# Half of the products of spectra and the filters' sums on GpSimd, the norms of some heads on ScalarE, and six more products of zeros

## The chip, the cores and the metric

The kernel runs on one core of one Trainium2 chip. The metric is the device time of one launch in microseconds, the median of 3 runs. Five engines take part: TensorE (PE for its products, PEld for its weight loads), VectorE (DVE), ScalarE (ACT), GpSimd (POOL) and SyncE (SP), which issues the loads.

## The reference

A two-layer encoder on 256 tokens of width 1024, in float32, with a memory of 256 tokens.

- Layer 0 mixes by a Hyena operator: the projected input goes through a short convolution over three neighbours, and then twice through `z = chunk * fftconv(z, filter)`. The filters come from a small network of sines over positions, and each is divided by the sum of the magnitudes of its taps. `fftconv` is a product of spectra: transform, multiply by the filter's spectrum, transform back.
- Beside it stands a cross attention of 4 heads of 128 to the memory. Queries and keys are normed head by head: each row's 128 numbers of a head are divided by the root of their mean square (`head_rms`).
- An output projection, a residual, and a SwiGLU of hidden width 2816 follow.
- Layer 1 mixes by dilated attention in three groups with the same head norms, again beside a cross attention, and ends in a mixture of 8 SwiGLU experts, of which each token takes 2.

## The kernel before

**Arithmetic.** Large products are done in three passes of a split number: each float32 operand is held as a high part (rounded by a ScalarE copy) and a low part (source minus high part, by a VectorE `tensor_tensor`, line 645, `split`). `mm3` (line 653) then does high*high, high*low and low*high. Every weight that is loaded goes through this split, in halves of 1024 columns (line 668, `weights`).

**Order of the work.** `Plan` (line 138) records every operation of the kernel. `flush` (line 588) then makes one list for nearly the whole kernel and emits it: `order` (line 397) gives each operation a due time by walking backwards through the graph, and then plays the engines forward with the durations of `cost` (line 321), taking at each engine the ready operation that is due first and for which buffers are free. So each engine's order is fixed when the kernel is built, and a changed operation or duration can change the order anywhere. Line 344 is what the planner assumes of a GpSimd `tensor_tensor`; it knows nothing of engines that hinder each other.

**The start.** `run` (line 851) sets up a tile of zeros and lets TensorE multiply it `WARM` times by itself, 128x128 in plain float32 (lines 881 to 884); these stand first on TensorE. In the trace each such product is two records. Then come the two products and the two sines of the filters' network (`taps`, line 899), which are due first on every engine, and the first dense block, the memory's keys of layer 0 (`memory`, line 1130).

**Head norms.** `heads_T` (line 748) norms the heads of a [2 x 128 tokens, 512] result that lies in PSUM, transposes them on TensorE and splits them. It is called four times: by `memory` for the keys of both layers, and by `cross` (line 802) for the queries of both. `head_norms` (line 726) does the norm: for each of two halves of the tokens one ScalarE Square over 512 columns and one VectorE reduction to 4 sums; then `rsqrt` (line 677, with a power on GpSimd over 8 columns); then for each half one VectorE product of 512 columns with the 4 factors broadcast. The dilated attention (`chunks`, line 1211) uses `head_norms` too.

**Filters and spectra.** `filters` (line 932) makes for each of the two filters the magnitudes of two tiles, adds them (line 956), and multiplies the sum by ones on TensorE to get the norm. `long_conv` (line 1043) takes the spectrum of its input and forms, for each of two halves r of the frequencies, four products of 512 columns with the filter's spectrum and from them a difference and a sum:

```python
for i, (f, g) in enumerate(((R[r], A[r]), (I[r], Dq[r]), (R[r], Dq[r]), (I[r], A[r]))):
    nc.vector.tensor_tensor(out=m[i], in0=f, in1=g, op=OP.mult)
nc.vector.tensor_tensor(out=m[0], in0=m[0], in1=m[1], op=OP.subtract)
nc.vector.tensor_tensor(out=m[2], in0=m[2], in1=m[3], op=OP.add)
```

The results are split and go back through TensorE. `long_conv` runs twice; between the two and after them stand the dense blocks of the projected input (`channels`, line 1002), whose convolution over neighbours is done by VectorE from PSUM, and whose results TensorE transposes (`channels_T`, line 1033).

Of the kernel before, what the change touches and what calls it, by code (L numbers as in the profile page):

```python
# [16 lines left out]
AF = mybir.ActivationFunctionType  # L17
OP = mybir.AluOpType
# [8 lines left out]
HD = 128  # L27
EPS = 1e-6
NB = 32
NUNIT = 33  # L30
WARM = 14


C_XQ, C_XK, C_AQ, C_AK = 0, 2, 4, 5
# [586 lines left out]
class _Kernel:  # L621
# [125 lines left out]

    def heads_T(self, ps, dst, scale=None, rms=None):

        zn = self.head_norms(ps, 0, 4, rms)  # L750
        d = dst.rearrange("p (h a t) -> p h a t", h=4, a=2)
        for a in range(2):
            p = self.bank()
            for h in range(4):
                self.tr(p[:, h * 128:(h + 1) * 128], zn[a][:, h * HD:(h + 1) * HD])
            self.split(d[:, :, a], p.rearrange("p (h t) -> p h t", h=4), scale=scale)
# [94 lines left out]
    def run(self):  # L851
# [30 lines left out]
        nc.vector.memset(idle, 0.0, kind="first")  # L882
        for _ in range(WARM):
            nc.tensor.matmul(ps[:, :128], lhsT=idle, rhs=idle, start=True, stop=True, kind="warm")
# [47 lines left out]
    def filters(self, hp, hm, w3, decay, skip, dft):  # L932

        nc = self.nc
        self.A, self.Dq, self.inv = [], [], []
        for o in range(2):
            at = slice(o * 512, (o + 1) * 512)
            P, Q, ab = [], [], []  # L940
            for t in range(2):
                pq = []
                for h, dst in ((hp, P), (hm, Q)):
                    ps = self.bank()
                    nc.tensor.matmul(ps, lhsT=h[:, t * 128:(t + 1) * 128], rhs=w3[:, at], start=True, stop=True)
                    pq.append(self.slot(512))
                    nc.vector.tensor_tensor(out=pq[-1], in0=ps, in1=decay[:, t * 512:(t + 1) * 512], op=OP.mult)
                    dst.append(pq[-1])

                mag = [self.slot(512) for j in range(2)]  # L950
                for j in range(2):
                    nc.scalar.activation(mag[j], pq[j], AF.Abs)
                ab.append(mag[0])
                nc.vector.tensor_tensor(out=ab[t], in0=mag[0], in1=mag[1], op=OP.max)
            ps, tot = self.bank(), self.slot(512)
            nc.vector.tensor_tensor(out=tot, in0=ab[0], in1=ab[1], op=OP.add)
            nc.tensor.matmul(ps, lhsT=self.ones, rhs=tot, start=True, stop=True)
            sk = self.slot(512)
            nc.vector.scalar_tensor_tensor(sk, ps, 1e-6, skip[:, at], op0=OP.add, op1=OP.mult)

            ps = self.bank()
            for j in range(4):
                nc.tensor.matmul(ps[:, j:j + 1], lhsT=tot[:, j * 128:(j + 1) * 128], rhs=self.ones[:, :1],
                                 start=True, stop=True)
            inv = self.tiny(4)
            nc.vector.tensor_scalar(inv, ps[:, :4], 1e-6, None, op0=OP.add)
            nc.vector.reciprocal(inv, inv)
            self.inv.append(inv)
            A, Dq = self.spectrum(dft, P, Q, sk)
            self.A.append(A)  # L970
            self.Dq.append(Dq)
# [71 lines left out]
    def long_conv(self, o, U, dft):  # L1043


        nc = self.nc
        R, I = self.spectrum(dft, U, U)
        A, Dq = self.A[o], self.Dq[o]
        Y = {}
        for r in (1, 0):  # L1050
            m = [self.slot(512) for i in range(4)]
            for i, (f, g) in enumerate(((R[r], A[r]), (I[r], Dq[r]), (R[r], Dq[r]), (I[r], A[r]))):
                nc.vector.tensor_tensor(out=m[i], in0=f, in1=g, op=OP.mult)
            nc.vector.tensor_tensor(out=m[0], in0=m[0], in1=m[1], op=OP.subtract)
            nc.vector.tensor_tensor(out=m[2], in0=m[2], in1=m[3], op=OP.add)
            Y[0, r], Y[1, r] = m[0], m[2]
        out = []
        for i in range(2):
            for r in range(2):
                out.append(self.pair(512))  # L1060
                self.split(out[-1], Y[i, r])
        return out
# [175 lines left out]
    def head(self, h, at, vecs, out):  # L1238

        nc = self.nc  # L1240

        bias = self.bias_of(vecs, h).rearrange("p (a s t) -> p a s t", a=2, s=4)
        q, k, v = ([at[f"{n}{g}", h] for g in range(3)] for n in "qkv")
        half = lambda p, a: p[:, a * 128:(a + 1) * 128]
        pT = self.pair(1024).rearrange("p (s a t) -> p s a t", s=4, a=2)
        for a in range(2):
            ps = self.bank()
            self.mm3(ps[:, :256], half(q[0], a), k[0], True, True)
            for g in (1, 2):
                self.mm3(ps[:, 128 + 128 * g:256 + 128 * g], half(q[g], a), half(k[g], a), True, True)  # L1250
            sc = self.slot(512)
            nc.vector.tensor_tensor(out=sc.rearrange("p (s t) -> p s t", s=4), in0=ps.rearrange("p (s t) -> p s t", s=4),
                                    in1=bias[:, a, :, ::-1], op=OP.add)
            g1 = lambda t: t.rearrange("p (z k) -> p z k", z=1)
            self.softmax_rows(g1(sc), 1, g1(sc))
            tp = self.bank()
            for s in range(4):
                self.tr(tp[:, s * 128:(s + 1) * 128], sc[:, s * 128:(s + 1) * 128])
            self.split(pT[:, :, a], tp.rearrange("p (s t) -> p s t", s=4))
        po = self.bank()  # L1260
        for s in range(2):
            self.mm3(po[:, :256], half(v[0], s), pT[:, s].rearrange("p a t -> p (a t)"), s == 0, False)
        for s in (2, 3):
            for a in range(2):
                self.mm3(po[:, a * 128:(a + 1) * 128], half(v[s - 1], a), pT[:, s, a], False, s == 3 and a == 1)
        self.split(out[:, h], po[:, :256])
# [380 lines left out]
```

## Time and profile before

| | us |
|---|---|
| median of 3 runs (lowest to highest) | 1317.12 (1317.06 to 1317.91) |
| the profiled execution, device time | 1316.6 |
| its span, first to last instruction | 1314.7 |
| PE busy | 1298.1 (99%) |
| PEld busy | 1073.8 (82%) |
| DVE busy | 1082.4 (82%) |
| ACT busy | 903.9 (69%) |
| POOL busy | 42.0 (3%), 38 instructions |

The span is 1.9 us shorter than the profiled execution's device time. The mean granted clock of TensorE over the span is 0.995 of the full one. A busy time is the time in which an engine had an instruction in work; matmuls are pipelined, and their ends are modelled, so neighbours overlap. Since all operations are emitted by one helper, nearly every row has line L301, and the operations are told apart by tile names and shapes: `b` is a PSUM bank, `s` a tile of SBUF, `tiny` a few columns of scalars, `kt` the constants, `x` the residual stream, `mhalf` the exponents of the power.

### The profile page before, as it was taken

The numbers are of one execution on the slowest core, as the hardware profiler recorded it, in microseconds if no ns is written. First come the engines' busy times: TensorE is split into PE (matmuls) and PEld (weight loads), VectorE is DVE, ScalarE is ACT, GpSimd is POOL, SyncE is SP. The second block draws the span as 40 slices with busy tenths as digits, with TensorE's granted clock in tenths as the row PEclk, the third lists the DMA queues.
The fourth block names the chain that finished last, engine by engine and source line by source line (L and its number), as shares of the span: only waits on it lengthen the run. The fifth ranks groups of instructions, "written<-read, shape, count | busy, mean of one in ns | idle before, by whom it ended". The sixth has DMA issues, their size and how long they took to land.

```text
span 1314.7 us, 16854 instructions
## 1 busy us (share of the span) xinstructions
PE 1298.1 (99%) x6236; PEld 1073.8 (82%) x6236; DVE 1082.4 (82%) x1434; ACT 903.9 (69%) x1185; POOL 42.0 (3%) x38
## 2 busy tenths in 40 slices
PE   7999999999999999999999999999999999999997
PEld 5798888888878888888888888888888888888885
DVE  7999765554578777899988999898998899989895
ACT  7455854444556565687777877777777777778884
POOL 1000000000001001000000000000000000000000
PEclk8999999999999999999999999999999999999998
DMA  9737534457434465388999998999998999999961
GB/s 364 297 129 288 225 119 140 152 186 268 166 132 173 157 212 222 115 347 330 346 411 417 336 381 323 372 421 384 359 373 308 397 380 422 336 381 370 354 264 18
DMA packets 57725, 373.82 MB, mean 284 GB/s; under 512 B 6447, under 2 KB 10627, under 8 KB 13988
## 3 DMA queue, kind: packets, MB, share of 16 engines
q1 hardware_dynamic: 56484, 368.48, 72.4%
q0 software_dynamic: 1152, 4.19, 1.8%
q8 instruction: 51, 0.84, 0.2%
q14 instruction: 38, 0.31, 0.1%
HBM read 366.86 MB, written 5.79 MB: 283 GB/s over the span
## 4 chain that ended last, share of the span: by engine, by line
PE 88%; issue 7%; DVE 3%; ACT 1%; DMA 1%; POOL 0%; POOLq 0%; ACTq 0%; DVEq 0%
PE b L301 88%; DVE s L301 3%; ACT s L301 1%; DMA out<-s,tiny 1%; DVE tiny L301 0%; POOL tiny L301 0%; POOL out L298 0%; DVE x L301 0%; POOLq L1387 0%; ACTq L301 0%; POOLq L298 0%; DVEq L301 0%
## 5 line engine op out<-in xcount | busy, mean ns | idle before, releaser
L301 PE MATMUL b<-s,s 128*128 128x512 f32 (+2 forms) x5678 | 1270.0, 382 | 6.4 <-ACT s L301 3.6
L301 PEld LDWEIGHTS b<-s,s 128*128 128x128 f32 (+1 forms) x5678 | 1009.0, 188 | 212.3 <-DVE s L301 6.7
L301 DVE TENSOR_TENSOR s<-s,s 128x1024 fp32r<-128x1024 f32 (+2 forms) x728 | 835.0, 1185 | 140.7 <-ACT s L301 137.9
L301 ACT CAST s<-s 128x1024 fp32r<-128x1024 f32 (+1 forms) x701 | 699.9, 1038 | 244.2 <-PE b L301 124.3
L301 DVE TENSOR_TENSOR s<-b,s 128x512 f32<-128x512 f32 (+5 forms) x214 | 127.6, 610 | 36.8 <-ACT s L301 32.3
L301 ACT CAST s<-b 128x512 fp32r<-128x512 f32 (+3 forms) x118 | 58.2, 502 | 55.7 <-PE b L301 53.6
L301 PE MATMUL b<-kt,s 128*128 128x128 f32 (+1 forms) x448 | 78.0, 271 | 0.4 <-ACT s L301 0.4
L301 PEld LDWEIGHTS b<-kt,s 128*128 128x128 f32 x448 | 58.6, 144 | 16.5 <-ACT s L301 1.3
L301 ACT ACTIVATE s<-b 128x512 f32<-128x512 f32 (+3 forms) x81 | 43.1, 536 | 23.7 <-PE b L301 18.6
L301 POOL TENSOR_TENSOR tiny<-tiny,mhalf 128x1 f32<-128x1 f32 (+4 forms) x23 | 28.6, 1246 | 323.3 <-DVE tiny L301 323.1
L301 ACT ACTIVATE s<-b,sm 128x256 fp32r<-128x256 f32 (+1 forms) x68 | 28.3, 484 | 13.1 <-PE b L301 12.5
L301 ACT ACTIVATE s<-b,tiny 128x256 f32<-128x256 f32 (+2 forms) x50 | 28.6, 598 | 12.3 <-PE b L301 11.7
L298 POOL DMA_INDIRECT out<-s,tiny x8 | 12.9, 1612 | 754.2 <-ACT s L301 658.5
L301 DVE SCALAR_TENSOR_TENSOR s<-b,sm,s 128x256 fp32r<-128x256 f32 (+1 forms) x72 | 31.1, 476 | 5.1 <-ACT s L301 4.9
L301 DVE TENSOR_REDUCE tiny<-s 128x4 f32<-128x512 f32 (+4 forms) x34 | 19.3, 586 | 7.7 <-ACT s L301 7.5
L301 ACT ACTIVATE s<-s,tiny 128x256 f32<-128x256 f32 (+1 forms) x32 | 18.4, 616 | 7.6 <-DVE tiny L301 7.6
L301 ACT ACTIVATE s<-x 128x512 f32<-128x512 f32 x16 | 10.1, 629 | 10.5 <-DVE x L301 9.8
L301 DVE TENSOR_TENSOR tiny<-tiny 128x1 f32<-128x1 f32 (+4 forms) x81 | 12.2, 157 | 4.5 <-POOL tiny L301 2.7
L301 PE MATMUL b<-s 128*128 128x128 f32 (+3 forms) x64 | 14.5, 349 | 1.1 <-DVE s L301 1.1
L301 ACT ACTIVATE s<-s 128x512 f32<-128x512 f32 (+2 forms) x14 | 8.2, 596 | 9.8 <-DVE s L301 9.8
L301 DVE TENSOR_TENSOR x<-b,x 128x512 f32<-128x512 f32 x12 | 8.3, 690 | 7.6 <-PE b L301 7.6
L301 DVE TENSOR_TENSOR s<-b,tiny 128x512 f32<-128x512 f32 (+3 forms) x26 | 13.7, 559 | 0.6 <-PE b L301 0.4
(67 smaller groups left out, 149.4 us busy)
## 6 DMA issues: line engine op xcount, KB each, us to landing
s<-w_moe SPq DMA_DIRECT2D x264, 1024.0 KB, 7.5
s<-w_ffn SPq DMA_DIRECT2D x33, 1024.0 KB, 4.9
s<-w_at SPq DMA_DIRECT2D x20, 1024.0 KB, 5.0
s<-w_kv SPq DMA_DIRECT2D x8, 1024.0 KB, 4.9
s<-w_hy SPq DMA_DIRECT2D x8, 1024.0 KB, 13.4
s<-w_out SPq DMA_DIRECT2D x8, 1024.0 KB, 5.3
s<-mem_t SPq DMA_DIRECT2D x4, 512.0 KB
out<-x SPq DMA_DIRECT2D x3, 512.0 KB, 2.7
```

Of the source, the lines that this page charges most:

```text
L298: self.nc.gpsimd.indirect_dma_start(out=out, out_offset=bass.IndirectOffsetOnAxis(ap=index, axis=0), in_=rows, in_offset=None, compute_op= ...
L301: getattr(getattr(self.nc, op.eng), op.fn)(*args, **kw)
```

## The change

Four edits. The number of products of zeros goes from 14 to 20. `heads_T` no longer calls `head_norms`: it squares each head by itself on ScalarE with the sum accumulated by the same instruction (8 instructions for 2), needs no VectorE reduction, and multiplies each head by its factor on ScalarE (8 instructions for VectorE's 2). The sum of the two magnitude tiles of each filter goes from VectorE to GpSimd. Of the four products of spectra the second and the fourth go to GpSimd.

```diff
-WARM = 14
+WARM = 20
     def heads_T(self, ps, dst, scale=None, rms=None):
-        zn = self.head_norms(ps, 0, 4, rms)
+        nc = self.nc
+        head = lambda t, h: t[:, h * HD:(h + 1) * HD]
+        ss = self.tiny(8)
+        for a in range(2):
+            kw = {} if rms is None else dict(scale=rms[a])
+            for h in range(4):
+                nc.scalar.activation(self.slot(HD), head(ps[a], h), AF.Square, accum_out=ss[:, 4 * a + h:4 * a + h + 1], **kw)
+        r = self.rsqrt(ss, 8, HD)
+        for a in range(2 if rms else 0):
+            nc.vector.tensor_scalar(r[:, 4 * a:4 * a + 4], r[:, 4 * a:4 * a + 4], rms[a], None, op0=OP.mult)
+        zn = [self.slot(512) for a in range(2)]
+        for a in range(2):
+            for h in range(4):
+                nc.scalar.activation(head(zn[a], h), head(ps[a], h), AF.Copy, scale=r[:, 4 * a + h:4 * a + h + 1])
         d = dst.rearrange("p (h a t) -> p h a t", h=4, a=2)
...
             ps, tot = self.bank(), self.slot(512)
-            nc.vector.tensor_tensor(out=tot, in0=ab[0], in1=ab[1], op=OP.add)
+            nc.gpsimd.tensor_tensor(out=tot, in0=ab[0], in1=ab[1], op=OP.add)
...
             for i, (f, g) in enumerate(((R[r], A[r]), (I[r], Dq[r]), (R[r], Dq[r]), (I[r], A[r]))):
-                nc.vector.tensor_tensor(out=m[i], in0=f, in1=g, op=OP.mult)
+                (nc.gpsimd if i % 2 else nc.vector).tensor_tensor(out=m[i], in0=f, in1=g, op=OP.mult)
```

## Rows read from the trace of the kernel before

**Rows 1.** Busy time by stage: us, each engine's busy time (instructions), PEclk, DMA.
```profile
24.80:33.70 8.90, 8.08 (x40) 5.23 (x39) 7.15 (x18) 8.68 (x14) 1.65 (x1) 1.00 1.02 406
33.00:130.00 97.00, 97.00 (x591) 83.26 (x590) 93.18 (x160) 51.66 (x80) 2.55 (x1) 1.00 0.61 234
62.00:84.50 22.50, 22.50 (x165) 21.36 (x163) 22.33 (x37) 10.94 (x17) 0.00 (x0) 1.00 0.14 47
```
**Rows 2.** Waits of PE from 24.9 to 1306: us, times, longest us.
```profile
PE b L301 <- DVE s L301: 1.2, 2, 0.7
PE b L301 <- ACT s L301: 0.4, 1, 0.4
```
**Rows 3.** Timeline of the start: start us, us, instruction, count [idle before].
```profile
4.78 1.17 PE L301 MATMUL b<-s 128*128 128x128 f32 x9
5.23 0.72 PE L301 MATMUL b<-s 128*128 128x128 f32 x5
6.56 0.53 DVE L301 TENSOR_SCALAR s<-b,sm 64x256 f32<-64x256 f32 x1 [2.52 <-PE b L301]
14.10 11.14 PE L301 MATMUL b<-s,s 128*128 128x512 f32 x40 [1.41 <-DVE s L301]
```
**Rows 4.** Busy time in three stretches of the start, columns as above.
```profile
6.54:9.45 2.91, 0.00 (x0) 0.00 (x0) 2.71 (x7) 1.51 (x3) 0.00 (x0) 1.00 1.04 435
11.07:17.88 6.81, 5.40 (x13) 3.72 (x13) 6.67 (x15) 6.81 (x17) 0.09 (x1) 0.50 1.01 374
17.90:24.80 6.90, 6.90 (x31) 5.69 (x31) 5.51 (x31) 4.84 (x12) 2.16 (x4) 1.00 1.02 421
```
**Rows 5.** Timeline of ACT at the first head norm.
```profile
24.88 0.69 ACT L301 ACTIVATE s<-b,tiny 128x512 f32<-128x512 f32 x1 [1.38 <-PE b L301]
...
26.99 1.15 ACT L301 ACTIVATE s<-x,tiny 128x1024 f32<-128x1024 f32 x1
```
**Rows 6.** Timeline of ACT: a Square of 128 columns; accumulating activations of 256.
```profile
503.60 0.28 ACT L301 ACTIVATE s<-b 128x128 f32<-128x128 f32 x1 [5.61 <-PE b L301]
...
130.08 0.47 ACT L301 ACTIVATE s<-b,tiny 128x256 f32<-128x256 f32 x1
...
130.53 0.47 ACT L301 ACTIVATE s<-b,tiny 128x256 f32<-128x256 f32 x1
```
**Rows 7.** Groups of DVE, 60 to 84.5: operation, shapes, count, busy us, mean ns.
```profile
L301 DVE TENSOR_TENSOR s<-s,s 128x512 f32<-128x512 f32 x12 | 7.7, 683 | 0.0
```
**Rows 8.** Groups of DVE, 24.8 to 33.8.
```profile
L301 DVE TENSOR_REDUCE tiny<-s 128x4 f32<-128x512 f32 x2 | 1.4, 686 | 2.4 <-ACT s L301 2.4
```
**Rows 9.** Timeline of the first long convolution.
```profile
67.60 3.09 DVE L301 TENSOR_TENSOR s<-s,s 128x512 f32<-128x512 f32 x5
...
81.17 3.21 DVE L301 SCALAR_TENSOR_TENSOR s<-b,tiny,s 128x255 f32<-128x255 f32 x8
...
84.50 0.63 PE L301 MATMUL b<-kt,s 128*128 128x128 f32 x4
```
**Rows 10.** Groups of POOL over the span.
```profile
L301 POOL TENSOR_TENSOR tiny<-tiny,mhalf 128x6 f32<-128x6 f32 x2 | 2.6, 1322 | 24.9 <-DVE tiny L301 24.9
...
L301 POOL TENSOR_TENSOR tiny<-tiny,mhalf 128x2 f32<-128x2 f32 x2 | 1.4, 696 | 15.9 <-DVE tiny L301 15.9
```
**Rows 11.** Timeline where POOL's power of 8 columns meets DVE.
```profile
112.39 1.22 DVE L301 TENSOR_TENSOR s<-s,s 128x1024 fp32r<-128x1024 f32 x1
112.56 2.55 POOL L301 TENSOR_TENSOR tiny<-tiny,mhalf 128x8 f32<-128x8 f32 x1 [81.81 <-DVE tiny L301]
...
406.94 1.65 POOL L301 TENSOR_TENSOR tiny<-tiny,mhalf 128x8 f32<-128x8 f32 x1 [29.44 <-DVE tiny L301]
407.10 2.35 DVE L301 TENSOR_TENSOR s<-s,s 128x1024 fp32r<-128x1024 f32 x2
```
**Rows 12.** Timeline at layer 0's cross attention: the norm's second product, first transposes.
```profile
119.36 0.68 DVE L301 TENSOR_TENSOR s<-b,tiny 128x512 f32<-128x512 f32 x1
119.47 0.60 PE L301 MATMUL b<-kt,s 128*128 128x128 f32 x4
```

## The prediction

> **What bounds the kernel now.** I read the busy times by stage first. From 33 to 130 us, the stage in which both long convolutions and both filters lie, PE is busy for all 97.00 us, and DVE for 93.18 of them; ACT has half of the stage free [rows 1]. So two engines are full side by side, and the question is which one waits for the other. The view of waits answers it: from 24.9 us to 1306 PE waits three times in all, 1.6 us together [rows 2], and the same view of 33 to 130 has no row for PE. PE is the bound, DVE runs just ahead of it. Work taken off DVE there buys nothing by itself; work added to DVE costs as soon as PE comes to wait. What an edit can still win lies in those 1.6 us and in the start, read from the timeline: DVE stands idle until the products of zeros and the first product behind them are through (6.56), and from there its queue leads to 14.10, where PE begins the first dense block after a wait of 1.41 us for DVE [rows 3]. In the start the clock also counts: PE did nothing from 6.54 to 9.45, and from 11.07 to 17.88 the granted clock was 0.50, 1.2 GHz, before it came back [rows 4].
>
> **Six more products of zeros.** Each is two records. Nine records from 4.78 and five from 5.23 end together, so four take 0.45 us, 0.112 each at full clock [rows 3]; twelve take 1.35 us. They stand first on PE, and behind them the product for the sines, DVE's sines, DVE's low parts and then the dense block at 14.10. DVE was busy for 2.71 of the 2.91 us after 6.54 [rows 4], so I find no cover: the block starts 1.35 us later. What it loses is less, since until 17.88 it ran at half the clock [rows 4]: 1.35 us of that time was worth 0.67 us of work. That holds if the clock falls as before, and I think it does: the pause of 2.9 us that stood before the fall [rows 4] is moved, not shortened. **+0.7.** Upper bound +1.35 (nothing absorbed); lower bound -1.9: the clock stays up, which gives back half of the 3.78 us from 14.10 to 17.88, and DVE fills the wait with a low part of the weights.
>
> **Head norms, four calls.** Each call takes two reductions (0.69 us) and two products (0.68) from DVE [rows 8, 12]; on a queue without pauses such an operation of 512 columns costs 0.60, five taking 3.09 with the overlap of the last [rows 9], so DVE gains 2.4 us a call. For ACT, a Square of 128 columns took 0.28 us, and accumulating activations of 256 columns with a pointer follow each other by 0.45 [rows 6]; the new Square lies between them, and I take 0.37, as 128 columns fewer than 256 save about 0.08 by the two rows. Eight make 3.0 us for 1.2 now (two of 0.60). The eight scaled copies I take at 0.33 (between the same rows), 2.6 us. So ACT gains 4.4 us of work a call, and a norm ends about 1.8 us later at its sums and 1.4 later at its copies. Of the calls, three have cover: the layer 0 queries (ACT half idle [rows 1], and the first transposes come at 119.47, in a PE queue with no wait [rows 12, 2]) and both of layer 1's, in stretches where PE waits 0.9 us in all [rows 2]. The first call has none: from 24.80 to 33.70 ACT is busy for 8.68 of 8.90 us [rows 1]. There ACT waits 1.38 us for the dense block, does the two Squares, and only then scales the second half of the rows of x (26.99) [rows 5], on which the next dense block hangs. If all eight Squares are put ahead of that, it is 1.8 us late; if it goes before them, PE's longest wait, 0.7 us, is won. With half of them ahead, 4 x 0.37 stand for 1.2: **+0.3**, bounds -0.7 and +1.8.
>
> **Sums of magnitudes and products of spectra: ten operations of 512 columns.** On DVE one takes 0.68 us [rows 7]. On GpSimd no row shows a plain one; its powers cost 0.696 us for 2 columns and 1.322 for 6 [rows 10], 0.157 a column and 0.38 fixed. Lower bound 0.68, DVE's own time for the same work; upper bound, at the power's slope, 0.38 + 512 x 0.157 = 80.8 us. A product of two tiles is nearer to DVE's row than to a power, so I take GpSimd's fixed 0.38 and, for 512 columns more, what DVE's operation of 1024 (1.22 [rows 11]) takes beyond one of 512, 0.54: 0.92 us.
>
> Does it run beside DVE? The power of 8 columns takes 1.65 us where it starts ahead of DVE's subtraction of two SBUF tiles, and 2.55 where that subtraction is already running [rows 11]: POOL waited for 0.9 us. In the other direction two such subtractions that start 0.16 us after the power take 2.35 as a pair, undisturbed [rows 11], but the power reads only 8 columns. The Trainium skill (SBUF — State Buffer, section "Who interferes with whom") says that a VectorE instruction with two SBUF inputs contends with a GpSimd instruction that reads SBUF, by a lock held for the whole instruction. The trace agrees for POOL's side; for DVE's side no row has a read long enough. By that page no product would run beside one of DVE's, by the pair at 407.10 alone all would. The skill's price (GPSIMD Engine Reference, section "Elementwise — side-by-side cycle accounting") is 1.96 times VectorE's, so an estimate of 1.34 us; the ten would then cost 13.4 us instead of 9.2.
>
> I reckon with the serial case from the rows. In the first long convolution DVE is full (22.33 of 22.50 [rows 1]), and nearly all of its work there has two SBUF inputs [rows 7, 9]. Four products leave DVE (-2.4) and block it for 4 x 0.92: +1.3 in each convolution; the two sums +0.6 together. The first norm has by then given DVE 2.4. So at 84.50, where PE's transposes follow DVE's convolution (81.17 + 3.21 = 84.38 [rows 9]), DVE stands at 1.3 + 0.6 - 2.4 = -0.5, not later than now; after the second convolution at +0.8, against the 3.8 us that it is idle from 33 to 130 [rows 1]. If the two run side by side, DVE gains and PE, which doesn't wait, does not. Either way **0**; below nothing there is nothing to win, and the upper side is the first rival. On POOL's own queue the powers of the norms stand behind the products, but the next one (112.56) comes after them.
>
> **Sum.** 1316.6 (the profiled execution; the median is 0.5 higher) + 0.7 + 0.3 + 0 = 1317.6, on the scale of the median 1318.1. A measurement of this kernel can tell about 0.2%, 2.6 us, from no change: that is 1314.5 to 1319.7.
>
> **Rivals.**
> - *DVE falls behind PE (slower).* The list is made with POOL and DVE side by side, and it spends what DVE gains by pulling other work forward. Each of a convolution's four POOL products then comes up to 0.92 us later than PE's order assumes, and the reads wait for one another: 1.3 to 3.7 us per convolution that PE has no order for, say 2.5 twice. 1317.6 + 5.0 + 0.5 = 1323.1. For it: the 0.12 us between 84.38 and 84.50, POOL's wait of 0.9, and that PE has hardly a wait to lose. Against: the 2.4 us from the norms, and that DVE has 3.8 us idle. It decides once DVE is more than some 0.1 us later at 84.38 than now. The page's lock gives this case at its dearer price, too.
> - *The start wins (faster).* The clock stays at 1.0 through 11.07 to 17.88 (-1.9), the row of 26.99 goes first (-0.7), and the two waits left in layers 0 and 1 go (-0.9): 1313.1 + 0.5 = 1313.6. Against: all three must come together to pass 0.2%.
> - *GpSimd multiplies at its power's pace (slower).* Four products of 80.8 us in each convolution would put some 600 us on the path, about 1900.
> - *It doesn't do what it says.* The zeros don't hold the clock, and DVE's free time is not PE's: that is my forecast.
>
> **Chances.** Forecast (no change) 0.47; DVE behind 0.39; start wins 0.12; the power's pace 0.02, left outside the range. Faster by over 0.2% 0.12, within 0.47, slower 0.41. The range goes from 1314.9, between forecast and the faster case, to 1323.4, just past the slower one; the forecast's own range is 1315.5 to 1319.7.
>
> **What would show it.** In the trace after: the dense block at about 15.4 instead of 14.10, and a stretch of clock 0.50 between 11 and 18 (right) or none (the faster rival). POOL's products of 512 columns with a duration near 0.9, DVE's subtractions beside them longer than 0.68 or 1.22 if the lock holds from DVE's side. PE's waits from 33 to 130: none (right) or several us behind DVE (the first rival). If the time is over 1320 with no such waits, or if the waits lie in layer 1, the order of the list moved something that I have not seen, and the reasoning was wrong even where the sign is right.

## The result and the profile after

The changed kernel takes 1324.99 us (median of 4, 1323.08 to 1327.66), the kernel before, beside it, 1317.51: ratio 1.0059, 95% interval 1.0046 to 1.0071. That is 7.5 us slower; 1318.1 was predicted, 1323.4 was the top of the range. The profiled execution of after has 1323.08 us and a span of 1321.3, so 6.5 us of the loss stand in its trace. It is the quickest of the four executions; what the others lose beyond it (1324.98 to 1327.66) no trace shows.

Busy times by stage of after, columns as in [rows 1]; the last row is the stretch of the start that answers to the second of [rows 4]:
```profile
24.80:33.70 8.90, 7.16 (x34) 4.43 (x32) 6.96 (x17) 8.24 (x24) 1.65 (x1) 1.00 1.02 410
33.00:130.00 97.00, 93.41 (x569) 79.57 (x568) 86.82 (x137) 56.80 (x109) 17.61 (x11) 1.00 0.54 206
62.00:84.50 22.50, 20.69 (x156) 19.70 (x155) 20.57 (x26) 11.91 (x17) 5.91 (x4) 1.00 0.24 89
10.72:17.53 6.81, 6.81 (x16) 4.90 (x17) 6.67 (x14) 6.43 (x15) 0.09 (x1) 0.50 1.01 367
```
From 33 to 130 PE was never idle before; now it is idle for 97.00 - 93.41 = 3.6 us, 1.8 of them in the first long convolution. DVE looks less busy, 86.82 us for 93.18, and yet PE waits for it. The stretch at clock 0.50 stands where it stood.

Waits of PE in after from 24.9 to 1306, columns as in [rows 2]:
```profile
PE b L301 <- DVE s L301: 5.9, 4, 1.8
PE b L301 <- ACT s L301: 0.6, 1, 0.6
PE b L301 <- DMA s<-onehot: 0.3, 1, 0.3
```
6.8 us for 1.6. Where they stand, from PE's timeline of after (start, us, instruction, count [idle before]):
```profile
32.70 0.38 PE L301 MATMUL b<-s,s 128*128 128x256 f32 x1 [1.74 <-DVE s L301]
...
75.80 10.21 PE L301 MATMUL b<-s,s 128*128 128x256 f32 x73 [1.81 <-DVE s L301]
...
107.40 0.97 PE L301 MATMUL b<-s,s 128*128 128x512 f32 x3 [1.78 <-DVE s L301]
...
380.76 2.88 PE L301 MATMUL b<-s,s 33*4 33x256 f32 x11 [0.27 <-DMA s<-onehot]
384.19 0.33 PE L301 MATMUL b<-kt,s 128*128 128x128 f32 x1 [0.55 <-ACT s L301]
```
One in the start (0.68 before), one in each long convolution (none before), two small ones where layer 1 begins. The sixth, 0.56 us at 514, stands in before, too. DVE's last addition to the residual in each of three stages says how much of the loss lies ahead of it. Before (layer 0's mix, its feed-forward, layer 1's mix):
```profile
153.69 0.68 DVE L301 TENSOR_TENSOR x<-b,x 128x512 f32<-128x512 f32 x1
...
351.19 1.37 DVE L301 TENSOR_TENSOR x<-b,x 128x512 f32<-128x512 f32 x2 [0.89 <-PE b L301]
...
534.74 0.69 DVE L301 TENSOR_TENSOR x<-b,x 128x512 f32<-128x512 f32 x1
```
After:
```profile
158.20 0.68 DVE L301 TENSOR_TENSOR x<-b,x 128x512 f32<-128x512 f32 x1
...
355.72 1.37 DVE L301 TENSOR_TENSOR x<-b,x 128x512 f32<-128x512 f32 x2 [0.67 <-PE b L301]
...
540.48 0.69 DVE L301 TENSOR_TENSOR x<-b,x 128x512 f32<-128x512 f32 x1
```
4.5 us later after layer 0's mix, as much after the feed-forward, 5.7 after layer 1's mix, 6.5 at the end. So two thirds lie in the first 158 us, and 2 us behind the feed-forward.

What GpSimd and DVE do there. Groups of POOL in after over the span, then of DVE from 60 to 84.5 (operation, shapes, count, busy us, mean ns, idle before):
```profile
L301 POOL TENSOR_TENSOR s<-s,s 128x512 f32<-128x512 f32 x9 | 14.7, 1654 | 51.8 <-DVE s L301 51.8
...
L301 DVE TENSOR_TENSOR s<-s,s 128x512 f32<-128x512 f32 x9 | 7.5, 873 | 0.7 <-ACT s L301 0.7
L301 DVE TENSOR_TENSOR s<-s,s 128x1024 fp32r<-128x1024 f32 x5 | 7.2, 1432 | 0.6 <-ACT s L301 0.6
L301 DVE TENSOR_TENSOR s<-b,s 128x512 f32<-128x512 f32 x6 | 3.9, 685 | 1.7 <-PE b L301 1.6
```
A GpSimd operation of 512 columns takes 1.65 us on the mean. DVE's operations with both inputs in SBUF take 873 and 1432 ns instead of 683 [rows 7] and 1.22 us [rows 11]; those that read one input from PSUM (s<-b,s) keep 685, two of them while GpSimd multiplies (POOL, then DVE, of after):
```profile
68.12 4.26 POOL L301 TENSOR_TENSOR s<-s,s 128x512 f32<-128x512 f32 x3 [18.45 <-DVE s L301]
...
68.71 1.29 DVE L301 TENSOR_TENSOR s<-b,s 128x512 f32<-128x512 f32 x2
```
Busy time of DVE holds the time in which it is shut out, so its share no longer tells how much it does. One place close up, all engines of after:
```profile
73.01 1.65 POOL L301 TENSOR_TENSOR s<-s,s 128x512 f32<-128x512 f32 x1 [0.63 <-DVE s L301]
73.45 2.89 DVE L301 TENSOR_TENSOR s<-s,s 128x1024 fp32r<-128x1024 f32 x2
73.79 1.04 ACT L301 CAST s<-s 128x1024 fp32r<-128x1024 f32 x1 [0.26 <-PE b L301]
75.80 0.89 PEld L301 LDWEIGHTS b<-s,s 128*128 128x128 f32 x7 [2.01 <-DVE s L301]
```
The first of DVE's two lasts 2.29 us, 1.07 more than undisturbed, and ends at 75.74; PE starts at 75.80. It is no operation of the convolution but a low part (128x1024, fp32r) of the dense work that PE does in between.

### The profile page after: what moved, and what is told of

It reads as the page before. It is cut to its first block, busy times and chain, and to the rows that moved or that the text cites. A ratio compares the mean times of both kernels' runs of the same rounds, so it can differ in the third digit from the quotient of the medians.

```text
span 1321.3 us, 16968 instructions
## 1 busy us (share of the span) xinstructions
PE 1302.7 (99%) x6248; PEld 1074.6 (81%) x6248; DVE 1075.6 (81%) x1408; ACT 917.4 (69%) x1273; POOL 59.2 (4%) x48
## 4 chain that ended last, share of the span: by engine, by line
PE 80%; issue 7%; DVE 2%; DMA 1%; ACT 1%; POOL 0%; POOLq 0%; DVEq 0%; ACTq 0%
PE b L301 80%; DVE s L301 2%; ACT s L301 1%; DMA out<-s,tiny 1%; DMA s<-onehot 1%; POOL out L298 0%; POOLq L1401 0%; DVE tiny L301 0%; DVEq L301 0%; POOLq L298 0%; ACTq L301 0%
## 5 line engine op out<-in xcount | busy, mean ns | idle before, releaser
L301 PEld LDWEIGHTS b<-s,s 128*128 128x128 f32 x5674 | 1009.1, 188 | 217.7 <-DVE s L301 11.2
L301 ACT ACTIVATE s<-b,tiny 128x128 f32<-128x128 f32 (+3 forms) x94 | 40.2, 482 | 9.5 <-PE b L301 6.0
L301 PE MATMUL b<-s 128*128 128x128 f32 (+3 forms) x80 | 17.3, 348 | 1.1 <-DVE s L301 1.1
L301 DVE TENSOR_REDUCE tiny<-s 128x1 f32<-128x512 f32 (+4 forms) x26 | 14.1, 557 | 4.2 <-ACT s L301 4.1
L301 POOL TENSOR_TENSOR s<-s,s 128x512 f32<-128x512 f32 x9 | 14.7, 1654 | 51.8 <-DVE s L301 51.8
L301 ACT COPY s<-b 128x512 f32<-128x512 f32 x11 | 6.5, 590 | 13.9 <-PE b L301 13.9
L301 DVE TENSOR_SCALAR tiny<-tiny 128x1 f32<-128x1 f32 (+4 forms) x70 | 11.2, 165 | 5.6 <-ACT s L301 4.6
```

The costliest lines, as they stand in the source:

```text
L301: getattr(getattr(self.nc, op.eng), op.fn)(*args, **kw)
```

## The experiments

Each time stands against the median of the kernel before on the same chip (1317.5 to 1318.1 us), with the 95% interval of the ratio behind it.

**The change cut in two.** e1 has the products on GpSimd and nothing else of the change, e4 everything but them.
```
-WARM = 20                      +WARM = 14          (e1; also the old head_norms
                                                     and the sum on nc.vector)
-(nc.gpsimd if i % 2 else nc.vector).tensor_tensor(...)     (e4)
+nc.vector.tensor_tensor(...)
```


> Of the change only the products of spectra on GpSimd; norms, sums and products of zeros as before. Theory A (GpSimd's reads and VectorE's two-input instructions shut each other out, VectorE falls behind TensorE in both convolutions): PE waits behind DVE of about 1.8 us in each convolution or a little more, since the norms no longer relieve DVE, and DVE instructions stretched by GpSimd's 1.3; +3.6 to +5 us, about 1321.5. Theory B (the list is made anew, and any new list costs a few us wherever it happens to): no special waits in the convolutions, about a third of the whole loss, +2.5 us, 1320.

> The whole change without the products of spectra, which stay on VectorE. Theory A: the two waits of 1.8 us in the convolutions are gone, what is left is the start (+1.0) and some 1 to 2 us behind it: 1318.5 to 1320. Theory B: two thirds of the loss stay, +5 us, 1322.5.

e1: 1323.34 us, +5.5 (1.0033 to 1.0059); waits behind DVE in the convolutions, 3.5 us in all. e4: 1319.72, +1.9 (1.0007 to 1.0025); none there. The products are most of the loss. The traces agree. The last addition of layer 0's mix, which stands at 153.69 in before and 158.20 in after, stands here in e4:
```profile
153.53 0.68 DVE L301 TENSOR_TENSOR x<-b,x 128x512 f32<-128x512 f32 x1
```
Up to there, in these executions, what e4 leaves of the change costs nothing. Its loss comes later: layer 1's mix ends at 537.39 for 534.74. Both carry a newly written order, so this alone doesn't say whether the chip or the order does it.

**What of a GpSimd operation shuts DVE out.** Three kernels leave the order of before on every engine as it is and put GpSimd work beside it, whose results nobody uses. d1 multiplies the two tiles of every second product once more; d2 and d3 read one column and write the rest with memsets, d2 in four places of a convolution, d3 in one.
```
+ for h in range(2):                                        (d1)
+     at = slice(h * 256, (h + 1) * 256)
+     pool.tensor_tensor(out=out, in0=x[:, at], in1=y[:, at], op=OP.mult)
...
+ pool.tensor_tensor(out=out[:, :1], in0=x[:, :1], in1=y[:, :1], op=OP.mult)
+ for h in range(24):                                       (d3; d2: 6)
+     pool.memset(out, 0.0)
```


> The kernel before with its list unchanged on every engine; only beside every second product of spectra GpSimd multiplies the same two tiles as well, in two halves of 256 columns, into a tile that nobody reads (eight times 512 columns in all). Theory A: DVE's two-input instructions are stretched by up to 1.3 us for each of the eight, PE waits behind DVE 2 to 4.5 us in each convolution, +4 to +9 us, about 1323.5. Theory B: the list is the same, so the time is too, 1317.3.

> As the kernel with the products beside, but GpSimd reads only one column of the two tiles and then fills its tile with zeros six times: it writes and does not read. Theory A (it is the reads): DVE's instructions keep their 0.68 and 1.22 us, no wait of PE in the convolutions, 1317.3. If it is GpSimd's activity as such, or its writes: stretched DVE instructions and waits as with the reads, +4 us or more.

> The list of before unchanged; in each convolution GpSimd reads one column once and then fills its own tile with zeros 24 times, so that no buffer of the convolution waits for it to come free, as it did where it read a column four times. If only GpSimd's reads hinder VectorE: no stretched DVE instruction, no PE wait in the convolutions, within 0.5 us of before (1317.5). If its writes do: DVE instructions over 0.68 and 1.22 us and a slower kernel, +2 us or more.

d1: 1325.16, +7.4 (1.0050 to 1.0076), with 5.9 us of waits of PE behind DVE in the convolutions. Groups of POOL, then of DVE, of d1 from 60 to 84.5:
```profile
L1075 POOL TENSOR_TENSOR spare<-s,s 128x256 f32<-128x256 f32 x8 | 7.9, 986 | 36.4 <-DVE s L301 35.9
...
L301 DVE TENSOR_TENSOR s<-s,s 128x512 f32<-128x512 f32 x12 | 10.9, 944 | 0.0
```
The same twelve DVE operations take 944 ns for 683 [rows 7]. d3: 1317.76 (0.9994 to 1.0012), nothing. The same groups of d3:
```profile
L1075 POOL MEMSET spare<- 128x256 f32 x24 | 7.5, 312 | 1.4
...
L301 DVE TENSOR_TENSOR s<-s,s 128x512 f32<-128x512 f32 x12 | 7.7, 685 | 0.0
```
GpSimd is busy for 7.5 us, about as long as in d1, but it writes only: DVE keeps 685 ns and PE has no wait from 33.9 to 130. So it is the reads that lengthen DVE's operations, not GpSimd's being at work nor its writes. d2: 1323.75 (1.0022 to 1.0051), its runs from 1318.15 to 1326.47. Its DVE operations are not longer either (684 ns), but PE waited once, 1.2 us at 83.71. I put that down to its one-column reads, which came as late as DVE let them, so that the tiles came free later; this is argued, not shown, and the traced execution (1320.43) is one of the quicker ones. So d2's time answers nothing about writes; d3, which reads once, does. And d1's 7.4 us may hold such a part, beside the lengthened operations.

**The products on GpSimd in the order of before.** The planner sees VectorE; only when an operation is written out does it go to GpSimd, in the same place. p1 moves eight, as the change does, p2 the last of each group of four.
```
+ at = nc.vector.tensor_tensor(out=m[i], in0=f, in1=g, op=OP.mult)
+ if i % 2:                                           (p2: if i == 3)
+     nc.swap[at] = "gpsimd"
...
+ op.eng = self.swap.get(op.i, op.eng)                (where it is written out)
```


> The order of the kernel before on every engine, with nothing else changed than that the second and fourth product of each group of four (eight in all) run on GpSimd, in the place of the list where VectorE had them. Theory (GpSimd's read of two tiles and VectorE's operations on two tiles shut each other out, whatever the list): GpSimd's products last 1.3 us or more, the VectorE operations beside them 1.2 to 1.8 us instead of 0.68, TensorE waits 1 to 2 us in each long convolution, and the time is 3.5 to 6 us above the kernel before. Rival (the new order that the planner wrote made the waits): no wait over 0.5 us in the convolutions and less than 1 us above.

> The order of the kernel before on every engine; only the fourth product of each group of four (four in all) runs on GpSimd, in the place that VectorE had it in. Theory (each GpSimd read of two tiles takes from VectorE about what the product on VectorE took, and the subtraction or sum behind it waits for the slower product): about half of what eight products cost in the same order, 2 to 3 us above the kernel before, with waits of TensorE of 0.5 us or more in the convolutions. Rival (one GpSimd operation per group hides beside VectorE's three, and only the second one of a group brings the wait): within 0.7 us of the kernel before and no wait over 0.3 us in the convolutions.

p1: 1322.83, +5.0 (1.0023 to 1.0050). Waits of PE from 33.9 to 130, and the groups of DVE in the first convolution, 69 to 76.5:
```profile
PE b L301 <- DVE s L301: 3.6, 3, 1.3
...
L301 DVE TENSOR_TENSOR s<-s,s 128x512 f32<-128x512 f32 x4 | 5.6, 1418 | 0.2
L301 DVE TENSOR_TENSOR s<-s,s 128x1024 fp32r<-128x1024 f32 x1 | 2.3, 2311 | 0.0
```
Four products left DVE there, 4 x 0.60 = 2.4 us. The five operations that stayed take (5.67 - 4 x 0.68) + (2.31 - 1.22) = 4.0 us longer. DVE is 1.6 us worse off for this convolution than with the products its own. The groups of the second one, 98.5 to 107.15:
```profile
L301 DVE TENSOR_TENSOR s<-s,s 128x1024 fp32r<-128x1024 f32 x2 | 4.6, 2306 | 0.0
L301 DVE TENSOR_TENSOR s<-s,s 128x512 f32<-128x512 f32 x3 | 3.1, 1046 | 0.0
L301 DVE TENSOR_TENSOR s<-s 128x512 f32<-128x512 f32 x1 | 1.8, 1778 | 0.0
```
By the same sum these six are 4.4 us longer, and DVE is 2.0 us worse off. In p1's trace layer 0's mix ends at 160.43, 6.7 us later than in before; 2.1 of them stand already at PE's transposes at 28.10 (25.99 in before), ahead of every product, and 4.6 behind them. p2: 1320.72, +2.6 (1.0013 to 1.0031), about half of p1, with 2.1 us of waits in the convolutions. Each GpSimd product costs, from the first on, and no new order is needed for it.

**The order of after without GpSimd.** s1 is the complement: the order that after was given, its eight products and the sums issued on VectorE in the places that the planner had for GpSimd.


> The order of the changed kernel on every engine, with the eight products and the sum of the magnitudes back on VectorE, in the places of the list that the planner gave them on GpSimd; head norms on ScalarE and twenty zero products stay. Theory (the reads shut each other out): the waits of 1.8 us at 75.8 and 107.4 us go, and the time is 1.5 to 3 us above the kernel before, as for the change without its products. Rival (the order did it): both waits stay, and it is 6 to 8 us above.

1323.89, +6.1 (1.0035 to 1.0059). No GpSimd read, and still PE waits 2.1 us behind DVE in the convolutions, for 3.6 in after. The time is the rival's (6 to 8), but the waits shrink, which neither side expected. The order counts on a DVE without these products, and has put other work where they were. By p1 a product on GpSimd costs DVE 1.0 us of waiting, and on DVE it costs 0.60, so I take it that DVE is over-full in this order either way; no run shows that by itself. Part of the 6.1 lies elsewhere: s1's trace has a stretch at clock 0.50 from 382.7 to 386.0, which the trace of after has not. At most half of it, some 1.7 us by estimate, is lost there.

**A planner that knows.** e5 is after, with a planner in which a GpSimd product waits for DVE's running operation and holds DVE until it ends.
```
+ reads = e == "gpsimd" and op.fn == "tensor_tensor" and op.dur > 1.0 and ...
+ if reads and busy["vector"] > t and op.i != self.force:
+     ...; asked = True; continue
...
+ if reads: busy["vector"], asked = max(busy["vector"], end), False
```


> The whole change, but the planner is told of the collision: when it plays the engines forward, a GpSimd product or sum of 512 columns waits for VectorE's running instruction and holds VectorE until it ends. Theory A, form 1 (the list is out of step: it has TensorE come for results that the lock makes late): with the lock in the list PE's two waits of 1.8 us go, and the time falls from 1325 to that of the change without the products, about 1320. Theory A, form 2 (VectorE has not the time, whatever the list): PE's waits stay or move within the convolutions, 1323 to 1325.

1325.88, +8.4 (1.0051 to 1.0079). The second convolution's wait shrinks (0.35 and 0.34 for 1.78), the first one's stays, 2.04 us. So this planner's knowing of it brought nothing back, as form 2 of the expectation has it for the waits; that DVE lacks the time is the reading I give it. e5's trace, too, has a stretch at 0.50, from 382.6 to 385.8.

**Heads and zeros.** e2 has only the norms of the change, e3 only the six products of zeros; both get a new order. w1 issues the six in the order of before.
```
+ nc.times[at] = 7          (w1: the last of the fourteen, written out seven times)
```


> Only the norms of heads_T on ScalarE. The whole change without the products was 1.9 us slower, with a PE wait of 1.73 us before the second dense block in place of 0.68. Theory A1: that wait is the norms' (all eight Squares stand ahead of the scaling of x): PE wait of about 1.7 us near 31 us, +1.0 to +1.5 us, 1319. Theory A2: it comes from the products of zeros, which delay the sines: then this one is within 0.3 us of before and its first wait is 0.7.

> Only twenty products of zeros instead of fourteen. By the prediction's step +0.7 us (1.35 us later, half of it absorbed while the clock is at 1.2 GHz): 1318.4. If they hold the clock up: 1316. If the later sines bring the wait of 1.7 us: 1319.

> The order of the kernel before on every engine; only six more products of the zero tile are issued behind the fourteen. If the zero products themselves cost what the first prediction said, the first product of the dense block comes some 1.3 us later, half of it is made good while the clock is at half, and the time is 0.7 us above the kernel before (0.3 to 1.3). Rival (the zero products cost what the kernel with them and a newly written order cost): 2 to 3 us above, with waits of TensorE of 1 us or more at about 12 and 32 us and near 379 us.

e2: 1319.60, +2.1 (1.0012 to 1.0030). e3: 1320.28, +2.8 (1.0014 to 1.0033). w1: 1318.79, +1.0 (1.0000 to 1.0017). The same zeros cost 2.8 with a new order and 1.0 without, and e4, which holds the norms and the zeros, costs 1.9, less than either alone. e2's trace has the wait near 31 us that theory A1 expected (1.49 us at 32.60, for 0.68), and besides 0.46 us in the convolutions and 1.20 us at 381.25. The timelines of the zeros, before, after and then w1:
```profile
1.06 5.47 PE L301 MATMUL b<-s 128*128 128x128 f32 x30 [1.06 <-DVE s L301]
...
1.06 6.64 PE L301 MATMUL b<-s 128*128 128x128 f32 x42 [1.06 <-DVE s L301]
...
1.06 8.01 PE L301 MATMUL b<-s 128*128 128x128 f32 x42 [1.06 <-DVE s L301]
```
Forty records are zeros and two the product behind them. The forty-two take 6.64 us in one execution and 8.01 in the other, so their price is itself uncertain by more than a microsecond. The thirty take from 5.33 (n1) to 6.85 (d2) in the traces of kernels that have fourteen zeros. Against the trace of before, w1's is 2.54 us later at the end of the zeros (8.01 for 5.47), at the dense block (16.64 for 14.10) and at the end of layer 0's mix (156.23 for 153.69): in these two executions nothing of the delay is made good. The stretch at clock 0.50, 11.07 to 17.88 in before, stands from 13.6 to 20.4 in w1. e3's loss shows elsewhere, in a trace that is its slowest execution (1322.08); three stretches of e3 (columns as above, PEclk third from the end):
```profile
372.00:378.90 6.90, 6.23 (x28) 3.91 (x26) 4.77 (x9) 5.28 (x7) 2.70 (x1) 1.00 0.34 140
378.96:385.76 6.80, 6.64 (x17) 4.49 (x18) 5.93 (x13) 1.69 (x3) 0.00 (x0) 0.50 0.02 4
385.80:392.00 6.20, 6.20 (x35) 5.24 (x33) 4.26 (x6) 1.64 (x2) 0.00 (x0) 1.00 0.51 171
```
PE waited 0.89 us for DVE up to 379.12, and from 378.96 on it ran 6.8 us at 0.50, 1.2 GHz: 17 records there, 35 in the shorter stretch at full clock behind it. The kernel before has no wait and no fall of the clock at that place. e4 has two falls in its trace, one behind its wait of 1.73 us at 31.43 and one behind a wait of 0.55 us for ACT at 379.51:
```profile
31.95:35.30 3.35, 3.35 (x18) 3.35 (x17) 1.29 (x3) 2.40 (x8) 0.00 (x0) 0.50 1.01 423
380.15:383.40 3.25, 3.25 (x11) 2.57 (x10) 3.25 (x7) 1.97 (x4) 0.00 (x0) 0.50 0.64 188
```
So of the ten traces with another order than before five have such a fall near 380 (e3, e4, s1, e5 and, below, n1), and no trace with the order of before has one.

**Orders with no change of work.** Three kernels change one constant of the planner each and nothing on any engine.
```
-HOLD = 20.0  +HOLD = 21.0    (n1)
-FREE = 0.2   +FREE = 0.25    (n3)
-SOON = 25.0  +SOON = 26.0    (n4)
```


> No engine gets other work: the one planner constant that gives operations off the dense chain their slack goes from 20.0 to 21.0, so that the planner writes another order. If the order of the kernel before is merely one of many equal ones, the time is within 0.5 us of it. If each newly written order costs by itself (the theory for the part of the loss that lies outside the convolutions), it is 0.5 to 3 us above, with a wait of TensorE of 0.5 us or more near 380 us that the kernel before does not have.

> No engine gets other work: the planner counts a buffer as free 0.25 instead of 0.20 us after its last use, and writes another order, different from row 49 of TensorE's list on. Theory (a newly written order costs by itself, by some microseconds that differ from order to order): 0.5 to 4 us above the kernel before, with new waits of TensorE outside the convolutions. Rival (the order with the slack at 21.0 was an unlucky one, others are equal): within 0.5 us.

> No engine gets other work: the planner may take up an operation 26 instead of 25 us ahead of when it is due, which leaves the order as it was through the convolutions and changes it behind them. Theory: the convolutions and all before them stay as in the kernel before (end of the layer's mix within 0.5 us of 151.94 us), a wait of TensorE of 0.5 us or more near 380 us is there, and the time is 0.5 to 3 us above. Rival (the loss of a new order lies at its start, ahead of the convolutions): within 0.5 us.

n1: 1321.56, +3.8 (1.0020 to 1.0044). n3: 1316.84 (0.9984 to 1.0002). n4: 1317.97 (0.9988 to 1.0006). My theory that a newly written order costs by itself falls: two of three cost nothing. But an order can cost almost 4 us. Around 379.44 in n1:
```profile
372.00:379.40 7.40, 6.99 (x31) 4.33 (x30) 5.64 (x12) 5.45 (x8) 2.70 (x1) 1.00 0.43 149
379.44:382.80 3.36, 3.36 (x10) 2.67 (x10) 3.36 (x8) 0.85 (x1) 0.00 (x0) 0.50 0.00 0
382.90:390.00 7.10, 7.10 (x38) 5.93 (x38) 5.67 (x8) 2.27 (x3) 0.00 (x0) 1.00 0.64 202
```
A wait of 0.46 us for DVE at 379.44, and 3.4 us at 0.50 from that moment. Of n1's 3.8 us this accounts, by estimate, for half of 3.4 us, 1.7, and the longer waits (2.7 us for 1.6 from 24.9 to 1306) another 1.1; the rest is not located.

No version beat the kernel before by more than its interval.

## Why the prediction was wrong

**The step that failed** is the end of the part on the ten operations: DVE "at 84.50 ... stands at -0.5, not later than now", therefore "either way 0". It measured +5.0 us in the order of before (p1), 3.6 of them as waits of PE in the convolutions.

- *What held.* That a GpSimd read and DVE's operations on two SBUF tiles hold each other up is shown: DVE's took 683 ns alone, 944 beside reads, 685 beside writes, and GpSimd's product 1.30 us alone, 1.65 on the mean. The Trainium skill (SBUF — State Buffer, section "Who interferes with whom") had it from both sides, and the runs agree; the pair at 407.10 [rows 11], which I let speak against it, only met a read of eight columns. Its condition of two SBUF inputs is borne out, too: 685 ns for those with one input in PSUM, beside a GpSimd product, too (68.71).
- *The price.* 0.92 us was estimated, from 0.68 up; undisturbed it is 1.30 (the first of the second convolution, at 96.98, 1301 ns), with waiting 1.65. The estimate of 1.34 by the Trainium skill's 1.96 times VectorE's (GPSIMD Engine Reference, section "Elementwise — side-by-side cycle accounting") was nearer than my 0.92. But DVE is held for less than that, 4.0 and 4.4 us by four in p1: 1.0 to 1.1 each. So the account of DVE, +1.3 us a convolution, was too low, but not by much; p1 has +1.6 and +2.0.
- *What was wrong is what I set against it.* First, I took one instruction, PE's transposes at 84.50, as the place where DVE's lateness shows. PE came to wait at 75.80, some nine microseconds earlier, for a low part of the dense work that DVE does between the products. On an engine that is full, every result for PE is due at its own time, and being late by 1.07 us at one of them is enough. Second, I credited the 2.4 us that the first head norm gives DVE and the 3.8 that it is idle up to 130. The gain was not there when it was needed: PE waits 3.5 us in the convolutions without the norms' relief (e1) and 3.6 with it (after). That the planner had spent it on pulling other work forward is the likely reason, but no run shows it. My first rival said just this, and set it beside a forecast that rested on the contrary.

**The other terms.** *Zeros +0.7:* the median says +1.0 (0.0 to 2.2) in the same order, but by luck, for neither half of the working is borne out. The delay in w1's trace is 2.54 us for 1.35, 0.21 for each of twelve records. I had taken 0.112 from records behind 4.78 [rows 3], while from 1.06 to 3.80 the same trace has 13 records in 2.74 us. And none of it is absorbed, as the stretch at 0.50 moves along with it. The dense block began not at 15.4: in after PE ran on from 10.63, as the new order has no wait there, and in w1 the block came at 16.64; a stretch at 0.50 stood in both, as forecast. *Head norms +0.3:* the Square took 0.37 us, as estimated, and the copies 0.27 apiece in a queue of eight, less than 0.33. But all eight Squares went ahead of the rows of x. ACT of after, first Square, last one, rows of x:
```profile
23.38 0.37 ACT L301 ACTIVATE s<-b,tiny 128x128 f32<-128x128 f32 x1 [1.47 <-PE b L301]
...
26.23 0.37 ACT L301 ACTIVATE s<-b,tiny 128x128 f32<-128x128 f32 x1
...
26.58 2.19 ACT L301 ACTIVATE s<-x,tiny 128x1024 f32<-128x1024 f32 x2
```
That is the case for which I had written +1.8; PE's wait grew from 0.68 to 1.74 us, +1.06. Norms alone cost 2.1 (e2) against 0.3; how much of it is the work and how much its order no run separates.

**The order itself** stood at nothing in the sum, with a sentence that a time over 1320 without waits in the convolutions would mean that "the order of the list moved something". It is a term: between -1.3 and +3.8 us in three orders with the same work. One place of its cost is seen, the falls of the clock near 380 in five of the ten other orders. p1's 5.0 and e4's 1.9 make 6.9 of the 7.5; the parts don't add exactly, as each has its own order. Where the last of it lies (0.8 us of drift behind 540 us among them) stays open.

**Of the rivals**, the first was right in sign and place, and in that the reads wait for one another (1.81 and 1.78 us of waits for "1.3 to 3.7 per convolution"), and came to 1323.1. That the traced execution has 1323.08 is luck in part: its waits in the convolutions are 3.6 us for the 5.0 of the rival's sum, and the rest is the start (1.06) and what lies behind the feed-forward. It was given 0.39, the forecast 0.47. On its side stood rows of my own: 0.12 us of room, and POOL's wait of 0.9.

## What to carry to other kernels

Moving an elementwise product of two SBUF tiles from VectorE to GpSimd relieved nothing here: it cost VectorE about 1.0 us in waiting for 0.6 us of work, on an engine whose results TensorE waits for. What GpSimd could do beside a full VectorE here without lengthening its operations was work that reads no SBUF, or one column of it; the room of a full engine is found at the first result that another one waits for, not at the end of the stage. And where a program writes the order, run some orders with unchanged work before a difference of 0.3% is put down to an edit.

## What the runs showed of the hardware

- GpSimd's memsets of 256 columns (0.31 us each, 48 of them) left VectorE as it was; its product of 256 columns, beside VectorE, took 0.99 us on the mean and lengthened VectorE's operations by 38%.
- Waits of TensorE of 0.89 us (e3) and 0.46 us (n1), both near 379 us, went with 6.8 and 3.4 us at clock 0.50; waits of 1.81 and 1.78 us in the convolutions of after left it at 1.00. The length of the wait alone does not decide: behind a wait of 1.73 us near 32 us the clock fell in e4, and behind one of 1.74 us at the same place of after it did not.
- The products of zeros run at two paces. From 1.06 to 3.80 us 13 records stand in after and in w1; from 3.90 to 6.70 there are 27 in after and 15 in w1. So the same 42 records took 6.64 or 8.01 us.
